# Two-layer pooling and stick-breaking trunk on one core: head sums by an accumulating transfer, and transposes of two blocks together

## The chip, the cores and the metric

The kernel runs on one core of one Trainium2 chip. The metric is device microseconds of one execution. Each core has TensorE (PE in the profile), VectorE (DVE), ScalarE (ACT), GpSimd (POOL) and SyncE (SP), each with a queue of its own that it works off in order, and 16 DMA engines that all queues share.

## The reference, cut to what matters

The input is `x` of 2048 frames by 1024 channels. Layer 0 is a gated pooling mixer; layer 1 is the attention that the change touches. Both end in a residual and a gated embedding ("PLE").

```python
q, z = jnp.split(rms_norm(x, b_norm[j]) @ b_w_in[j], 2, axis=-1)
q = rms_norm(split_heads(q), b_q_norm[j])            # 16 heads of 64
o = stick_breaking_attention(q, k_sh, v_sh)
x = x + (o * jax.nn.silu(z)) @ b_w_out[j]            # output projection
x = x + (p[i] @ ple_w[i]) * jax.nn.sigmoid(x @ ple_gate_w[i])

# stick-breaking, strictly causal, per head:
# A[t,s] = beta[t,s] * prod_{s<j<t} (1 - beta[t,j]),  beta = sigmoid(q.k / 8)
```

## The kernel before, in words

Layer 0 and the projections to q, k and v fill the first half of the span (lines before 855); nothing of them is touched. From about 1345 us the attention runs in four stretches, one for each chunk `c` of 512 queries, in the order 3, 2, 1, 0. A chunk has 16 heads, and each head goes over the key chunks `kc` from `c` down to 0. Such a (chunk, head, key chunk) is a slot: 64, 48, 32 and 16 slots in the four stretches.

A slot is worked in four steps `n`, one for each block of 128 queries. Three lags run side by side in one loop (from line 1197):

- `front` (L917 to L941), at step n: two matmuls (L924, L925) give the logits of a block in `psl`, ACT makes `kap`, the sigmoid of minus the logits (L928), and DVE runs the product along the keys into `pp` (a scan, L936, or L933 for the diagonal slot, whose blocks are 128, 256, 384 and 512 wide).
- `turn` (L943 to L954), six steps later: PE transposes up to four 128x128 pieces of `pp` into one PSUM tile `psa` (L949, pool of two buffers), ACT copies it to `at` (L952), and DVE stores the rest that the copy rounds off (L953).
- `gather` (L956 to L981), eight steps after `front`: two matmuls (L961, L962) with stored differences of v add to `pso`.

After a head's last gather ACT copies the two halves of `pso` to `ob` and `os` (L976, L977; the two products of a head lie in different halves of the partitions). For the second head of a pair DVE adds `ob` to `os` (L979), ACT adds a bias in four pieces (`gated`, L972), POOL multiplies by the gate `zt` that SP loaded (L974), and ACT and POOL later split the result into the pair `og` (L1006, L1007) for the output projection. These are put off by `soon(k, ...)`, which runs its function k steps later.

Beside the attention a generator feeds dense matmuls (L994, L996, L998), a few at each step: the gate projection `gate_z` (DVE L1028, ACT L1032, POOL L1033), and `post(c)`, which does the output projection, the gate and the embedding of the chunk that is just finished (DVE L1068 and L1109, POOL L1076 and, for chunks 3 and 2, POOL's accumulating transfer to the output, L1119). `shares` spreads the dense matmuls over the steps of a stretch by a cost model; `even` is a constant rate for the later stretches. `stops[c]` is the step at which chunk c is expected to be done. When all eight `os` of a chunk are appended, the rest of the filler is emptied and the next one begins. After the loop `post(0)` runs alone.

Instructions are put in order engine by engine by a scheduler that may shift those that are not held by `keep_in_program_order`, so small shifts of unrelated instructions come with any edit.

Of the kernel before, what the change touches and what calls it, by code (L numbers as in the profile page):

```python
# [30 lines left out]
def f(ap):  # L31
    return ap.bitcast(F32)
# [3 lines left out]
def trunk_kernel(ctx, tc, x, xt, pt0, wut, cols, heads, zin, grp, aout, agate, aple,  # L36
# [819 lines left out]
    with ExitStack() as st:  # L856
# [20 lines left out]
        def soon(k, fn):  # L877

            if tail[0]:
                fn()  # L880
                return lambda: None
            item = (now[0] + k, len(due), fn)
            due.append(item)

            def force():
                if item in due:
                    due.remove(item)
                    fn()

            return force  # L890
# [52 lines left out]
        def turn(st, kt):  # L943

            j0 = kt if st["diag"] else 0
            pt = psa.tile([P, W5], F32, tag="psa", name="psa")
            for j in range(j0, 4):
                pp, r0 = st["a"][j]
                T.transpose(pt[:, j * P : (j + 1) * P], pp[:, r0 + kt * P : r0 + (kt + 1) * P], ident)  # L949
            at = t2.tile([P, 2, W5], F32R, tag="at", name="at", bufs=3)  # L950
            cs = slice(j0 * P, W5)
            A.copy(out=at[:, 0, cs], in_=pt[:, cs])  # L952
            V.tensor_tensor(out=at[:, 1, cs], in0=pt[:, cs], in1=f(at[:, 0, cs]), op=ALU.subtract)  # L953
            st["at"][kt] = at  # L954

        def gather(st, kt):  # L956
# [6 lines left out]
            if st["last"] and kt == 3:  # L963
# [12 lines left out]
                soon(1, lambda: stay(A.copy(out=ob[mine], in_=po[other])))  # L976
                soon(2, lambda: stay(A.copy(out=os[mine], in_=po[mine])))  # L977
                if half:
                    soon(3, lambda: V.tensor_tensor(out=os, in0=os, in1=ob, op=ALU.add))  # L979
                    soon(4, gated)  # L980
                    soon(6, lambda: outs[c].append(os))  # L981

        def dense():
            if tail[0] and tail[0] % 4:
# [58 lines left out]

        def post(c):

            pin = t2.tile([P, 2, W5], F32, tag="pin", name="pin", bufs=1)
            nc.sync.dma_start(out=pin, in_=pt0[1, :, c * W5 : (c + 1) * W5].rearrange("(k q) n -> q k n", q=P))
            x3, og, held = [], ogs[c], tc.keep_in_program_order
            while len(og) < 8:
                pair_up(c)  # L1050
            settle()
            both = []
            for o in range(KT):
                xr = t2.tile([P, W5], F32, tag="tmp", name="xr", bufs=4)
                if not c and o < 2:
                    if not o:
# [23 lines left out]
            pt_ = []  # L1080
            for k in range(2):
                pr = t2.tile([P, 2, W5], F32R, tag="ple", name="ple")
                held(A.copy(out=pr[:, 0], in_=pin[:, k]))
                held(V.tensor_tensor(out=pr[:, 1], in0=pin[:, k], in1=f(pr[:, 0]), op=ALU.subtract))
                pt_.append(pr)
            yield
            made()
# [89 lines left out]
        AHEAD = 4  # L1177
        stops = {}
        for n, (c, _, _) in enumerate(slots):
            stops[c] = 4 * (n + 1) + LAG_G + 6  # L1180
        share, even = shares(0, stops[NSUB - 1], NSUB * POSTZ - HELD), 0.0
        done = set()
        ends = {}
# [12 lines left out]

        for n in range(4 * len(slots) + LAG_G):
            now[0] = n
            i2, j2 = divmod(n - LAG_T, 4)
            if 0 <= i2 < len(slots):  # L1200
                turn(active[i2], j2)
            i, j = divmod(n, 4)
            scan = None
            if i < len(slots):
# [37 lines left out]
        for _ in filler:  # L1242
# [54 lines left out]
```

## Time and profile before

| what | value |
|---|---|
| median of three runs | 2690.03 us (2689.37 to 2690.28) |
| the profiled execution's own time | 2688.62 us |
| its span, first to last instruction | 2686.8 us |
| granted TensorE clock, mean over the span | 0.999 |
| PE, DVE, ACT, POOL busy, share of the span | 99%, 72%, 52%, 34% |

The profiled execution's time is 1.8 us above its span. In the page, PE is the row of matmuls and PEld that of the weight loads, which go ahead of their matmuls. The ends of matmuls are modelled, so the distance from one matmul's start to the next says more than its duration. In the view of the waits a row gives the total, the number and the longest of the waits of one line for another.

### The profile page before, as it was taken

How to read it: one execution, taken by the hardware profiler on the slowest of the kernel's cores; microseconds unless marked ns; L12 is line 12 of the kernel's file. 1: busy time of each engine (PE TensorE's matmuls, PEld its weight loads, DVE VectorE, ACT ScalarE, POOL GpSimd, SP SyncE). 2: the span in 40 equal slices, each digit the busy share in tenths (PEclk: the TensorE clock that was granted, in tenths of full speed). 3: DMA queues.
4: the chain of work that ended last, by engine and by line, in shares of the span. 5: the costliest groups of instructions: out<-in, count | busy, mean ns of one | idle time of the engine just before them, and what ended most of it. 6: DMA issues, size and time to landing. Idle time of an engine off the chain costs nothing.

```text
span 2686.8 us, 38640 instructions
## 1 busy us (share of the span) xinstructions
PE 2671.1 (99%) x13352; PEld 2226.1 (83%) x13352; DVE 1926.8 (72%) x2490; ACT 1399.7 (52%) x2735; POOL 909.1 (34%) x724
## 2 busy tenths in 40 slices
PE   9999999999999999999999999999999999999999
PEld 7888888888888888888888888888888888888887
DVE  6776625666357643755499999999999998886632
ACT  6445623455135541445366666666666666665531
POOL 2674338643485434853221111022111111212220
PEclk9999999999999999999999999999999999999999
DMA  8657695567856678443778665555666677768965
GB/s 327 221 176 270 253 308 185 190 237 255 305 176 227 233 249 311 149 151 134 231 231 287 194 208 173 167 169 174 211 183 183 180 211 217 212 204 266 268 222 172
DMA packets 278992, 585.76 MB, mean 218 GB/s; under 512 B 33382, under 2 KB 67430, under 8 KB 278796
## 3 DMA queue, kind: packets, MB, share of 16 engines
q1 hardware_dynamic: 270754, 571.41, 64.6%
q10 hardware_dynamic: 5738, 7.68, 1.1%
q0 software_dynamic: 2304, 4.20, 1.0%
q8 instruction: 106, 1.74, 0.3%
q14 instruction: 90, 0.74, 0.1%
HBM read 438.40 MB, written 136.38 MB: 214 GB/s over the span
## 4 chain that ended last, share of the span: by engine, by line
PE 93%; DVE 4%; DMA 1%; ACT 1%; issue 0%; POOL 0%; SPq 0%; ACTq 0%; DVEq 0%
PE psd L614 19%; PE psd L166 9%; PE psd L167 9%; PE psd L168 9%; PE psa L949 8%; PE psd L994 6%; PE psd L998 6%; PE psd L996 6%; PE psl L925 4%; PE pso L962 4%; PE pso L961 4%; PE psl L924 4%; DVE pp L936 2%; DVE at L953 1%; PE pst L719 1%; PE psdt L994 1%
## 5 line engine op out<-in xcount | busy, mean ns | idle before, releaser
L952 ACT CAST at<-psa 128x512 fp32r<-128x512 f32 (+3 forms) x640 | 334.8, 523 | 430.3 <-PE psa L949 420.7
L614 PE MATMUL psd<-wpair,x 128*128 128x512 f32 x2304 | 536.8, 391 | 0.0
L936 DVE TENSOR_TENSOR_SCAN pp<-kap,pp,zeros 128x512 f32<-128x512 f32 x384 | 512.9, 1336 | 7.5 <-ACT kap L928 6.3
L614 PEld LDWEIGHTS psd<-wpair,x 128*128 128x128 f32 x2304 | 429.9, 188 | 87.0
L953 DVE TENSOR_TENSOR at<-psa,at 128x512 fp32r<-128x512 f32 (+3 forms) x640 | 382.5, 598 | 92.5 <-ACT at L952 87.5
L928 ACT ACTIVATE kap<-psl 128x512 f32<-128x512 f32 (+3 forms) x640 | 344.9, 539 | 13.0 <-PE psl L925 10.1
L949 PE MATMUL psa<-ident,pp 128*128 128x128 f32 x2176 | 344.1, 273 | 4.4 <-DVE at L953 3.8
L949 PEld LDWEIGHTS psa<-ident,pp 128*128 128x128 f32 x2176 | 266.0, 140 | 69.2 <-DVE at L953 12.4
L924 PE MATMUL psl<-kk,qa 128*128 128x512 f32 (+3 forms) x640 | 282.3, 441 | 0.0
L962 PE MATMUL pso<-at,vv 128*128 128x512 f32 (+3 forms) x640 | 234.6, 367 | 1.3 <-DVE at L953 1.3
L925 PE MATMUL psl<-kk,qb 128*128 128x512 f32 (+3 forms) x640 | 232.9, 364 | 0.0
L961 PE MATMUL pso<-at,vv 128*128 128x512 f32 (+3 forms) x640 | 232.7, 364 | 0.1
L933 DVE TENSOR_TENSOR_SCAN pp<-kap,ahead 128x128 f32<-128x128 f32 (+3 forms) x256 | 225.2, 880 | 5.2 <-ACT kap L928 3.2
L167 PE MATMUL psd<-xp,wpair 128*128 128x512 f32 x512 | 199.5, 390 | 1.9 <-DVE xp L316 1.9
L166 PE MATMUL psd<-xp,wpair 128*128 128x512 f32 x512 | 199.8, 391 | 0.8 <-ACT xp L315 0.8
L168 PE MATMUL psd<-xp,wpair 128*128 128x512 f32 x512 | 199.3, 390 | 0.0
L149 DVE SCALAR_TENSOR_TENSOR wpair<-wraw,gains,wpair 128x512 fp32r<-128x512 f32 x192 | 162.5, 888 | 46.6 <-ACT wpair L148 46.1
L143 POOL TENSOR_TENSOR wpair<-wraw,wpair 128x512 fp32r<-128x512 f32 x99 | 144.9, 1473 | 82.0 <-ACT wpair L141 77.4
L148 ACT ACTIVATE wpair<-wraw,gains 128x512 fp32r<-128x512 f32 x192 | 132.9, 719 | 70.2 <-DMA wraw<-in_bq_dram 31.7
L1033 POOL TENSOR_TENSOR zr<-zr,sgz 128x512 f32<-128x512 f32 x32 | 62.0, 1938 | 307.0 <-ACT sgz L1032 273.8
L141 ACT CAST wpair<-wraw 128x512 fp32r<-128x512 f32 x148 | 89.8, 619 | 120.1 <-PE psd L168 89.5
L962 PEld LDWEIGHTS pso<-at,vv 128*128 128x128 f32 x640 | 120.3, 188 | 27.6 <-DVE at L953 1.7
(201 smaller groups left out, 5333.1 us busy)
## 6 DMA issues: line engine op xcount, KB each, us to landing
kk<-kd SPq DMA_DIRECT2D x320, 128.0 KB
vv<-vd SPq DMA_DIRECT2D x160, 256.0 KB
wraw<-in_kv_dram SPq DMA_DIRECT2D x128, 256.0 KB
wpair<-wzd SPq DMA_DIRECT2D x64, 512.0 KB
wpair<-wod SPq DMA_DIRECT2D x64, 512.0 KB
wpair<-wgd SPq DMA_DIRECT2D x64, 512.0 KB
wpair<-wu SPq DMA_DIRECT2D x48, 512.0 KB
wpair<-wi SPq DMA_DIRECT2D x36, 512.0 KB
```

The lines of the kernel that those rows point to most:

```text
L166: T.matmul(ps, wst(units, kt, 0, c0), acts[kt][:, 0], start=(begin and kt == order[0]), stop=False)
L167: T.matmul(ps, wst(units, kt, 0, c0), acts[kt][:, 1], start=False, stop=False)
L168: T.matmul(ps, wst(units, kt, 1, c0), acts[kt][:, 0], start=False, stop=(end and kt == order[-1]))
L614: T.matmul(pss2[i], ck["x2"][kt][:, xh, tk], wst(ws, kt, wh, 0, W5), start=(kt == 0 and xh == 0 and wh == 0), stop=(kt == KT - 1 and wh == 1))
L924: T.matmul(ps[:, :w], qa[:, qs], kk[:, :w], start=True, stop=False)
L925: T.matmul(ps[:, :w], qb[:, qs], kk[:, :w], start=False, stop=True)
L928: A.activation(out=kp[:, r0:], in_=ps[:, :w], func=AF.Sigmoid, scale=-1.0)
L936: V.tensor_tensor_scan(out=pp[:, ::-1], data0=kp[:, ::-1], data1=zeros.to_broadcast([P, W5]), initial=st["carry"][j], op0=ALU.mult, op1=AL ...
L949: T.transpose(pt[:, j * P : (j + 1) * P], pp[:, r0 + kt * P : r0 + (kt + 1) * P], ident)
L953: V.tensor_tensor(out=at[:, 1, cs], in0=pt[:, cs], in1=f(at[:, 0, cs]), op=ALU.subtract)
L961: T.matmul(po[:, cs], vv[:, kt, :], at[:, 0, cs], start=(st["diag"] and kt == 0), stop=False)
L962: T.matmul(po[:, cs], vv[:, kt, :], at[:, 1, cs], start=False, stop=(st["last"] and kt == 3))
```

## The change

Four edits stand in the diff.

1. For chunks 3 and 2 the DVE addition L979 is replaced by a transfer on POOL's queue that adds `ob` to `os` in SBUF (new L980). `gated` then comes 6 steps after the head's end in place of 4, and the appending of `os` 8 in place of 6. Chunks 1 and 0 keep the addition (new L982). `stops` and the constant rate for chunk 1 follow the two steps.
2. From step `by_two` = 464 on, which is the end of chunk 2's last pair, `turn` is called for two blocks at each even step and for none at odd ones. A block with an odd number is thereby transposed one step earlier than before; the gathers stay where they were.
3. `at` gets four buffers in place of three.
4. The embedding input `pin` has no tile of its own any more: it takes two buffers of the four-buffer ring `tmp`, and is loaded by two transfers before the seventh of eight output projections, in place of one transfer at the start of `post`.

```diff
-            at = t2.tile([P, 2, W5], F32R, tag="at", name="at", bufs=3)
+            at = t2.tile([P, 2, W5], F32R, tag="at", name="at", bufs=4)
...
-                    soon(3, lambda: V.tensor_tensor(out=os, in0=os, in1=ob, op=ALU.add))
-                    soon(4, gated)
-                    soon(6, lambda: outs[c].append(os))
+                    if c > 1:
+                        soon(3, lambda: nc.gpsimd.dma_start(out=os, in_=ob, accum_op=ALU.add))
+                    else:
+                        soon(3, lambda: V.tensor_tensor(out=os, in0=os, in1=ob, op=ALU.add))
+                    soon(6 if c > 1 else 4, gated)
+                    soon(8 if c > 1 else 6, lambda: outs[c].append(os))
...
-            pin = t2.tile([P, 2, W5], F32, tag="pin", name="pin", bufs=1)
-            nc.sync.dma_start(out=pin, in_=pt0[1, :, c * W5 : (c + 1) * W5].rearrange("(k q) n -> q k n", q=P))
...
+                if o == KT - 2:
+                    pin = [t2.tile([P, W5], F32, tag="tmp", name="pin", bufs=4) for _ in range(2)]
+                    for k in range(2):
+                        nc.sync.dma_start(out=pin[k], in_=pt0[1, k * P : (k + 1) * P, c * W5 : (c + 1) * W5])
...
-            stops[c] = 4 * (n + 1) + LAG_G + 6
+            stops[c] = 4 * (n + 1) + LAG_G + (8 if c > 1 else 6)
+        by_two = stops[2] // 2 * 2
...
-            i2, j2 = divmod(n - LAG_T, 4)
-            if 0 <= i2 < len(slots):
-                turn(active[i2], j2)
+            for m in (n,) if n < by_two else (n, n + 1) if n % 2 == 0 else ():
+                i2, j2 = divmod(m - LAG_T, 4)
+                if 0 <= i2 < len(slots):
+                    turn(active[i2], j2)
...
-                        even = POST / (64.0 * c - (LAG_G + 2 if c == 1 else 1))
+                        even = POST / (64.0 * c - (LAG_G + 2 if c == 1 else 3))
```

Lines from 979 on carry numbers 3 to 6 higher in the changed kernel; L1035 and L1036 there are L1032 and L1033 here, L1010 is L1007, L997, L999 and L1001 are L994, L996 and L998, L1114, L1118 and L1119 are L1109, L1113 and L1114.

Three places show how instructions move. The first is the end of the second head pair of chunk 3. On ACT before, the bias L972 stands two `kap` behind the copy L977:

```order
L977 COPY os<-pso 64x512
L952 CAST at<-psa 128x512
L928 ACTIVATE kap_12444<-psl 128x512
L952 CAST at<-psa 128x512
L928 ACTIVATE kap_12445<-psl 128x512
L972 ACTIVATE os<-os,en 128x128 x4
```

On ACT in the changed kernel at the same place:

```order
L977 COPY os<-pso 64x512
L952 CAST at<-psa 128x512
L928 ACTIVATE kap_12444<-psl 128x512
L952 CAST at<-psa 128x512
L928 ACTIVATE kap_12445<-psl 128x512
L952 CAST at<-psa 128x512
L928 ACTIVATE kap_12442<-psl 128x512
L1035 ACTIVATE sgz<-zr 128x512
L952 CAST at<-psa 128x512
L928 ACTIVATE kap_12443<-psl 128x512
L972 ACTIVATE os<-os,en 128x128 x4
```

The bias stands four `kap` behind the copy now, two steps later.

On POOL, further on in chunk 3 (`og` is the pair for the output projection, `zr` and `sgz` belong to the gate projection), before:

```order
L1007 TENSOR_TENSOR og<-os,og 128x512
L1033 TENSOR_TENSOR zr<-zr,sgz 128x512
L974 TENSOR_TENSOR os<-os,zt 128x512
L1007 TENSOR_TENSOR og<-os,og 128x512
L1033 TENSOR_TENSOR zr<-zr,sgz 128x512
```

and in the changed kernel:

```order
L1010 TENSOR_TENSOR og<-os,og 128x512
L980 DMA os<-ob 128x512
L1036 TENSOR_TENSOR zr<-zr,sgz 128x512
L974 TENSOR_TENSOR os<-os,zt 128x512
L1010 TENSOR_TENSOR og<-os,og 128x512
L1036 TENSOR_TENSOR zr<-zr,sgz 128x512
```

The new transfer stands ahead of a multiplication that does not belong to it. Of the 16 new transfers, seven are followed by such an instruction and nine by their own L974.

The second place is PE in chunk 1, before:

```order
L949 MATMUL psa<-ident,pp 128x128 x4
L924 MATMUL psl<-kk,qa 128x512
L925 MATMUL psl<-kk,qb 128x512
L994 MATMUL psd<-og,wpair 128x512
L996 MATMUL psd<-og,wpair 128x512
L998 MATMUL psd<-og,wpair 128x512
L961 MATMUL pso<-at,vv 128x512
L962 MATMUL pso<-at,vv 128x512
L949 MATMUL psa<-ident,pp 128x128 x4
```

and in the changed kernel:

```order
L949 MATMUL psa<-ident,pp 128x128 x8
L924 MATMUL psl<-kk,qa 128x512
L925 MATMUL psl<-kk,qb 128x512
L1001 MATMUL psd<-og,wpair 128x512
L997 MATMUL psd<-og,wpair 128x512
L999 MATMUL psd<-og,wpair 128x512
L961 MATMUL pso<-at,vv 128x512
L962 MATMUL pso<-at,vv 128x512
L924 MATMUL psl<-kk,qa 128x512
L925 MATMUL psl<-kk,qb 128x512
```

Two groups of four transposes stand in one run of eight, and the next step begins with its logits.

The third place is DVE at the end of the attention, where the last `at` of chunk 0 are made beside the end of `post(1)` (`sg`, `x`: its gate and its sum), before:

```order
L953 TENSOR_TENSOR at<-psa,at 128x384
L1109 TENSOR_TENSOR sg<-psd,sg 128x512
L953 TENSOR_TENSOR at<-psa,at 128x256
L1114 TENSOR_TENSOR sg<-sg,x_26312 128x512
L953 TENSOR_TENSOR at<-psa,at 128x128
```

and in the changed kernel:

```order
L953 TENSOR_TENSOR at<-psa,at 128x384
L1114 TENSOR_TENSOR sg<-psd,sg 128x512
L953 TENSOR_TENSOR at<-psa,at 128x256
L953 TENSOR_TENSOR at<-psa,at 128x128
L1119 TENSOR_TENSOR sg<-sg,x_26318 128x512
```

The last `at` stands ahead of the sum that waits for POOL, no longer behind it.

More of the change, by code (lines that the diff above doesn't have):

```diff
@@ L1082, in post @@
                 pr = t2.tile([P, 2, W5], F32R, tag="ple", name="ple")
-                held(A.copy(out=pr[:, 0], in_=pin[:, k]))
-                held(V.tensor_tensor(out=pr[:, 1], in0=pin[:, k], in1=f(pr[:, 0]), op=ALU.subtract))
+                held(A.copy(out=pr[:, 0], in_=pin[k]))
+                held(V.tensor_tensor(out=pr[:, 1], in0=pin[k], in1=f(pr[:, 0]), op=ALU.subtract))
                 pt_.append(pr)
```

## Prediction

> **What bounds the kernel now.** I read the page first, for the engines and the chain that ended last.
>
> ```profile
> span 2686.8 us, 38640 instructions
> PE 93%; DVE 4%; DMA 1%; ACT 1%; issue 0%; POOL 0%; SPq 0%; ACTq 0%; DVEq 0%
> ```
>
> PE carries 93% of the chain. The number of matmuls does not change, so the change can only win what PE loses by waiting. Where that is, the view by windows tells, asked for the stretches of chunks 3, 2 and 1 (columns: window, length, then PE, PEld, DVE, ACT and POOL busy with their counts, clock, DMA share, GB/s).
>
> ```profile
> 1345.00:1870.00 525.00, 521.74 (x2881) 434.71 (x2880) 510.77 (x610) 340.70 (x680) 88.88 (x48) 1.00 0.64 201
> 1870.00:2210.00 340.00, 338.53 (x1882) 283.81 (x1881) 326.58 (x399) 225.00 (x466) 55.67 (x37) 1.00 0.64 192
> 2210.00:2435.00 225.00, 224.73 (x1250) 190.47 (x1249) 196.32 (x259) 146.75 (x324) 41.32 (x31) 1.00 0.75 216
> ```
>
> In chunks 3 and 2 (the first two rows) DVE is busy for 97% and 96% of the time, in chunk 1 for 87%, and PE never stands still for long. So DVE and PE run nearly level in chunks 3 and 2, and PE alone bounds chunk 1. Next the waits of PEld for DVE, asked for steps 1405 to 1870 us, 1870 to 2210 us, for 1870 to 1880 us and 2120 to 2210 us alone, and for the end from 2435 us; no such row answers for 2210 to 2435 us.
>
> ```profile
> PEld psa L949 <- DVE at L953: 5.0, 11, 1.6
> ```
> ```profile
> PEld psa L949 <- DVE at L953: 4.9, 9, 0.9
> ```
> ```profile
> PEld psa L949 <- DVE at L953: 1.6, 2, 0.9
> ```
> ```profile
> PEld psa L949 <- DVE at L953: 2.7, 5, 0.7
> ```
> ```profile
> PEld pso L962 <- DVE at L953: 1.7, 1, 1.7
> ```
>
> A wait in this view is longer than what PE loses, since loads run ahead. The longest one, in the timeline, gives the correction:
>
> ```profile
> 1780.43 0.39 PE L962 MATMUL pso<-at,vv 128*128 128x512 f32 x1
> 1781.28 0.67 DVE L953 TENSOR_TENSOR at<-psa,at 128x512 fp32r<-128x512 f32 x1
> 1782.00 0.42 PEld L949 LDWEIGHTS psa<-ident,pp 128*128 128x128 f32 x4 [1.61 <-DVE at L953]
> ```
>
> The transposes start 1.57 us after L962, where a matmul of this width takes 0.23 us from start to start (2354.33 to 2354.56 below). PE lost 1.34 us, the view says 1.61: 0.27 us too much for each wait. So PE lost 5.0 - 11 x 0.27 = 2.0 us in chunk 3 after 1405 us, 4.9 - 9 x 0.27 = 2.5 us in chunk 2, and 1.4 us at the end. That is about 6 us, and almost all that edits 1 and 2 can win.
>
> **The addition taken from DVE.** The addition and the steps around one of them, in chunk 3:
>
> ```profile
> L979 DVE TENSOR_TENSOR os<-os,ob x32: 659/669/1711, 1414.1 to 2585.1; 128x512 f32<-128x512 f32 x32
> 1588.61 0.58 ACT L977 COPY os<-pso 64x512 f32<-64x512 f32 x1
> 1589.96 0.60 ACT L928 ACTIVATE kap<-psl 128x512 f32<-128x512 f32 x1
> 1591.56 1.27 DVE L936 TENSOR_TENSOR_SCAN pp<-kap,pp,zeros 128x512 f32<-128x512 f32 x1
> 1591.79 0.60 ACT L928 ACTIVATE kap<-psl 128x512 f32<-128x512 f32 x1
> 1592.28 0.40 ACT L972 ACTIVATE os<-os,en 128x128 f32<-128x128 f32 x1
> 1871.50 1.71 POOL L1033 TENSOR_TENSOR zr<-zr,sgz 128x512 f32<-128x512 f32 x1 [0.45 <-ACT sgz L1032]
> 1872.05 1.71 DVE L979 TENSOR_TENSOR os<-os,ob 128x512 f32<-128x512 f32 x1
> ```
>
> DVE is rid of 16 x 0.67 us and of the 1.04 us by which the one at 1872 us was stretched beside POOL: 11.7 us. PE gets only what it waits for, and no single removal is worth more to it than its own length. Chunk 3 has eight additions in 525 us, and the two kinds need not meet: of its 2.0 us I count three quarters, 1.5 us, since the 1.34 us at 1780 us are worth one addition's 0.67 us at the most; of the 1.6 us from 1870 to 1880 us, right behind the stretched addition, all 1.1 us that PE lost. Of the five waits from 2120 us on (2.7 - 5 x 0.27 = 1.35 us) I count half, 0.7 us, since scans that POOL stretched (below) stand among their causes. Sum: 3.3 us gained, between nothing and 4.5 us.
>
> By the Trainium skill, SBUF — State Buffer, section "Who interferes with whom", a DVE instruction with two SBUF inputs and a GpSimd instruction that reads SBUF hold each other up, and the first to start has its way. The 1.71 us of L979 beside L1033 agrees with it.
>
> **The accumulating transfer in its place.** ACT must not reach L972 before it lands, since `kap` and the copies to `at` are queued behind L972, and DVE and PE behind those. The only accumulating transfers of before go to HBM:
>
> ```profile
> L1119 POOL DMA_DIRECT2D out_dram<-sg x16: 859/878/1095, 2040.1 to 2430.9; - x16
> DMA to landing us min/median/max: 4.4/5.5/7.7
> ```
>
> L977 ends at 1589.19. L972 comes two `kap` later than before; two of them are 1.83 us apart, so it is due at 1592.28 + 2 x 1.83 = 1595.94, which is 6.75 us after the copy. A landing takes 4.4 to 7.7 us, median 5.5, so the slot holds it in most cases. The latest would be 0.95 us late, and that is still covered: the `kap` that begins at 1589.96 ends at 1590.56, and its scan starts at 1591.56, so DVE runs 1.0 us behind ACT. I take a cost of 0. If POOL is held by an L1033 of 1.71 us ahead of the issue and the landing is the slowest, it is 9.4 us against 7.75: 1.7 us lost. Nothing excludes a landing that is quicker than these rows; it would bring nothing.
>
> The Trainium skill's page DMA: Bandwidth & Descriptors, section "Anatomy of one DMA — SWDGE (gpsimd) path", gives 2.0 us and bytes over 436 GB/s, an estimate of 2.6 us for these 256 KB; the measured 5.5 us is twice that, and the sum goes by the measured one.
>
> The issue itself costs DVE something in some cases. Two issues of L1119, each followed at once by L1007:
>
> ```profile
> 2100.97 0.87 POOL L1119 DMA_DIRECT2D out_dram<-sg  x1 [3.96 <-ACT kap L928]
> 2101.19 1.22 DVE L933 TENSOR_TENSOR_SCAN pp<-kap,ahead 128x512 f32<-128x512 f32 x1
> 2101.61 1.88 POOL L1007 TENSOR_TENSOR og<-os,og 128x512 fp32r<-128x512 f32 x1
> 2121.47 0.88 POOL L1119 DMA_DIRECT2D out_dram<-sg  x1 [17.98 <-PE psa L949]
> 2121.69 2.81 DVE L933 TENSOR_TENSOR_SCAN pp<-kap,ahead 128x384 f32<-128x384 f32 x1
> 2122.08 1.59 POOL L1007 TENSOR_TENSOR og<-os,og 128x512 fp32r<-128x512 f32 x1
> ```
>
> The first scan, 512 wide, took 1.22 us and the second, only 384 wide, 2.81 us: at least 1.6 us more. So an issue with a POOL instruction right behind it can hold a scan. Of the new issues seven have a foreign POOL instruction behind them; by ACT's order only in some four of these its input is ready at once. In chunk 2 the five waits from 2120 us on cost PE 1.35 us, 0.27 us apiece. Four such cost 1.1 us, none costs 0, all seven twice as much each 3.8 us; I take 0.7 us.
>
> **Two blocks transposed together.** What a group costs is read from PE's starts, one group of one and one of four:
>
> ```profile
> 2346.24 0.27 PE L949 MATMUL psa<-ident,pp 128*128 128x128 f32 x1
> 2346.27 0.36 PE L924 MATMUL psl<-kk,qa 128*128 128x256 f32 x1
> 2346.47 0.28 PE L925 MATMUL psl<-kk,qb 128*128 128x256 f32 x1
> 2346.59 0.40 PE L998 MATMUL psd<-x,wpair 128*128 128x512 f32 x1
> 2353.66 0.60 PE L949 MATMUL psa<-ident,pp 128*128 128x128 f32 x4
> 2354.01 0.48 PE L924 MATMUL psl<-kk,qa 128*128 128x512 f32 x1
> 2354.33 0.39 PE L925 MATMUL psl<-kk,qb 128*128 128x512 f32 x1
> 2354.56 0.39 PE L996 MATMUL psd<-x,wpair 128*128 128x512 f32 x1
> ```
>
> One transpose: 0.03 us to L924, and L924 takes 0.20 us where L925 of the same width takes 0.12, together 0.11 us. Four: 0.35 us, and L924 takes 0.32 us against 0.23, together 0.44 us, again 0.11 apiece. A group has no price of its own, so the 91 pairs save PE nothing. They might cost: both `psa` buffers must be free at once. Two steps lie between a buffer's uses, 3.5 us (chunk 1's 225 us hold 128 steps), and the second block's stores end about one copy (0.52 us) and one L953 (0.67 us) later than before; chunk 1 has 13% of DVE's time free, which hides it. I take 0; with that cover gone, 0.1 us in each of 91 pairs would be 9 us. An advantage is excluded by the rows, but for the end:
>
> ```profile
> L952 ACT CAST at<-psa 128x512 fp32r<-128x512 f32 (+3 forms) x640 | 334.8, 523 | 430.3 <-PE psa L949 420.7
> 2582.60 0.69 DVE L1114 TENSOR_TENSOR sg<-sg,x 128x512 f32<-128x512 f32 x1 [1.90 <-POOL sg L1113]
> 2583.21 0.28 DVE L953 TENSOR_TENSOR at<-psa,at 128x128 fp32r<-128x128 f32 x1
> ```
>
> The last L953 stands behind L1114, which waits 1.90 us for POOL. In the changed order it stands ahead of it, and the 1.4 us go. Late next is the chain of the last two blocks itself, two copies and two L953 of 0.3 to 0.4 us that gathers of 0.8 us cover in part: 0.2 us. Gain 1.2 us, between 0.5 and 1.7.
>
> **Buffers and loads.** The fourth `at` buffer only holds what the earlier transposes make. The `pin` loads move on SP behind the weights of the sixth projection. Their two `tmp` buffers last held `xr` of projections three and four, done two projections before, and their data are used three projections later; the ring leaves `xr` one projection of prefetch. Both 0, with a PE wait for `xr` as the price of failure; a stretch with DVE at 97% would show it.
>
> **Sum.** 3.3 + 1.2 - 0.7 = 3.8 us. The profiled execution, 2688.6 us (1.8 us above its span), would come to 2684.8, and the median, 1.4 us higher, from 2690.0 to **2686.2 us**.
>
> **Rivals.**
>
> *All of it goes.* If DVE's 11.7 us open so much room that no wait is left in chunks 3 and 2 and at the end, 2.0 + 2.5 + 1.4 = 5.9 us, with the waits ahead of 1405 us one or two more: about 2683.5. For it: DVE and PE run within 3 to 4% of each other. Against: waits behind stretched scans remain.
>
> *The work comes back on DVE.* If POOL's issues hold scans (1.6 us x 7 = 11.2 us against 11.7 us saved), chunks 3 and 2 stay as they are and only the end is won: 2690.0 - 1.2, about 2689. The two rows of L1119 speak for both.
>
> *The transfer lands late*, which ends slower. ACT stands at L972, `kap` behind it, DVE runs dry after its 1.0 us, then PE. The turning point is a mean landing of 7.75 us after the copy. At 9 us it costs 16 x 1.25 = 20 us, less 4.5 gained: about 2705. The median landing of 5.5 us speaks against it; that POOL can be 1.7 us late, and that DMA engines are 64% busy, for it. The Trainium skill's SBUF — State Buffer, section "SBUF: two separate sides", warns that a DVE instruction of a two-port mode keeps GpSimd from writing descriptors (0.62 us becoming 3.1 us). The issues of L1119 took 0.86 to 1.10 us in stretches with DVE 87 to 96% busy, so the trace does not bear it out for this DVE work.
>
> *The change does nothing measurable besides*, because scheduling shifts give back what it wins: 2690, with the forecast in the same class.
>
> **How the numbers follow.** The forecast has 0.45, the full gain 0.2, the two cases near 2689 to 2690 together 0.22, the late landing 0.13. What a measurement of this kernel can tell from no change is about 0.2%, 5.4 us. Faster by that needs under 2684.7: the full gain and the lower edge of the forecast, 0.22 in all. Slower needs over 2695.4: the late landing, 0.11 of its 0.13. Same has 0.67. The range goes from 2681.5 (all gains and the waits ahead of 1405 us) to 2692 (the work back on DVE and a lost microsecond or two); the late landing beyond it and edges are the 2 in 10 left out.
>
> **What would show it.** Right: no L979 in DVE's rows before 2200 us, DVE's busy time there 10 us down; PEld's waits for L953 falling from 9.9 to about 4 us between 1405 and 2210 us; ACT idle ahead of L972 near nothing; eight transposes in about 0.83 us to the next L924; no wait at the last L962. Wrong: an ACT wait for the transfer at L972; scans of 2 us and more beside the new issues; PE waits for `psa` between 2210 and 2435 us.

## The result and the profile after

The changed kernel took 2683.89 us (median of 12 runs, 2681.82 to 2685.63) and the kernel before 2689.26 us beside it (12 runs, 2688.38 to 2690.28): a ratio of 0.9979, 95% interval 0.9971 to 0.9986, or 5.4 us. In a second comparison (11 runs against 21) it was 2683.19 against 2688.93 us, 0.9976 (0.9967 to 0.9985). The forecast was 3.8 us less, with 2681.5 to 2692.0 as its range.

The page of the profiled execution answers to that of before with its span and its chain:

```profile
span 2682.4 us, 39425 instructions
PE 96%; DMA 1%; DVE 1%; issue 0%; ACT 0%; SPq 0%; ACTq 0%; DVEq 0%
```

DVE has fallen from 4% of the chain to 1%, and PE carries what DVE gave up. The windows, with the columns of before:

```profile
1345.00:1870.00 525.00, 521.11 (x2884) 435.09 (x2882) 507.98 (x603) 340.92 (x681) 91.60 (x56) 1.00 0.67 204
1870.00:2210.00 340.00, 339.89 (x1899) 286.83 (x1898) 317.64 (x394) 227.71 (x473) 61.44 (x45) 1.00 0.70 200
2210.00:2435.00 225.00, 224.66 (x1248) 192.45 (x1247) 195.44 (x258) 143.17 (x320) 41.63 (x31) 1.00 0.75 215
```

DVE is busy 2.8 us less in the first row and 8.9 us less in the second. PE's share rises in the second row alone, where its work of 340 us now leaves 0.1 us free in place of 1.5. The waits of PEld for DVE say the same, first for 1405 to 1870 us, then for 1870 to 2210 us:

```profile
PEld psa L949 <- DVE at L953: 4.0, 6, 1.0
```
```profile
PEld psa L949 <- DVE at L953: 0.8, 2, 0.4
```

Less 0.27 us for each wait, chunk 3 has 4.0 - 6 x 0.27 = 2.4 us where it had 2.0, and chunk 2 has 0.8 - 2 x 0.27 = 0.3 us where it had 2.5. Uncorrected that is 4.8 us, where the prediction named about 4. So the gain of the attention lies in chunk 2, and chunk 3 gave none. From 2210 to 2435 us, where no row of this kind stood before, there is one now:

```profile
PEld psa L949 <- DVE at L953: 0.7, 1, 0.7
```

The prediction named such a wait as a sign of being wrong. Edit 1 alone has it too (0.6 us in two waits), so the pairs do not make it.

The transfers (L980) and the bias behind them (L972), each asked by its line:

```profile
L980 POOL DMA_DIRECT2D os<-ob x16: 862/878/1092, 1414.1 to 2176.1; - x16
DMA to landing us min/median/max: 3.3/4.2/8.3
```
```profile
  DMA os<-ob: 1.4, 1
```

Fifteen of the 16 landed before ACT came to L972; one kept ACT waiting, 1.4 us, which is the other sign of that kind. At the end of the attention, DVE and PE in the timeline:

```profile
2577.27 0.69 DVE L1114 TENSOR_TENSOR sg<-psd,sg 128x512 f32<-128x512 f32 x1 [2.20 <-ACT sg L1100]
2578.04 0.62 DVE L953 TENSOR_TENSOR at<-psa,at 128x256 fp32r<-128x256 f32 x2
...
2578.74 0.22 PE L961 MATMUL pso<-at,vv 128*128 128x128 f32 x1
2578.80 0.27 PE L962 MATMUL pso<-at,vv 128*128 128x128 f32 x1
...
2580.23 0.69 DVE L1119 TENSOR_TENSOR sg<-sg,x 128x512 f32<-128x512 f32 x1 [1.57 <-POOL sg L1118]
```

Both of the last L953 (x2) end before the sum that waits for POOL, and the last L962 follows its L961 by 0.06 us, where before it had waited 1.28 us.

To place the difference, I compare two marks on PE: the first logits of the attention and the last matmul of the kernel, before and after (both kernels have 13352 matmuls).

```profile
1332.78 0.22 PE L924 MATMUL psl<-kk,qa 128*128 128x128 f32 x1
...
2681.50 0.39 PE L998 MATMUL psd<-ple,wpair 128*128 128x512 f32 x1
```
```profile
1333.08 0.22 PE L924 MATMUL psl<-kk,qa 128*128 128x128 f32 x1
...
2677.37 0.39 PE L1001 MATMUL psd<-ple,wpair 128*128 128x512 f32 x1
```

That distance went from 1348.7 to 1344.3 us, 4.4 us less. It leaves out what differs in the profiled executions ahead of the attention and in the last output. In the table below it is split at the start of step 255 (the end of chunk 3) and of step 512 (in chunk 1, past chunk 2's post-processing). Where a kernel appends two steps later, dense matmuls have moved behind these marks; their number, four at step 255 and five at step 512, was counted in the trace and 0.23 us added for each. Where pairs are made there, one more transpose stands ahead of step 512, and 0.11 us is taken off for it.

### The profile page after: what moved, and what is told of

It reads as the page before. It is cut to its first block, busy times and chain, and to the rows that moved or that the text cites. A ratio compares the mean times of both kernels' runs of the same rounds, so it can differ in the third digit from the quotient of the medians.

```text
span 2682.4 us, 39425 instructions
## 1 busy us (share of the span) xinstructions
PE 2669.6 (100%) x13352; PEld 2230.8 (83%) x13352; DVE 1907.9 (71%) x2474; ACT 1397.0 (52%) x2735; POOL 919.7 (34%) x740
## 4 chain that ended last, share of the span: by engine, by line
PE 96%; DMA 1%; DVE 1%; issue 0%; ACT 0%; SPq 0%; ACTq 0%; DVEq 0%
PE psd L614 19%; PE psd L167 9%; PE psd L166 9%; PE psd L168 9%; PE psa L949 9%; PE psd L997 6%; PE psd L1001 6%; PE psd L999 6%; PE psl L925 5%; PE pso L962 5%; PE psl L924 5%; PE pso L961 5%; PE pst L719 1%; PE psdt L997 1%; PE psdt L1001 1%; PE psdt L999 1%
## 5 line engine op out<-in xcount | busy, mean ns | idle before, releaser
L952 ACT CAST at<-psa 128x512 fp32r<-128x512 f32 (+3 forms) x640 | 325.5, 523 | 350.1 <-PE psa L949 340.0
L953 DVE TENSOR_TENSOR at<-psa,at 128x512 fp32r<-128x512 f32 (+3 forms) x640 | 375.0, 598 | 70.0 <-ACT at L952 64.7
L949 PE MATMUL psa<-ident,pp 128*128 128x128 f32 x2176 | 329.3, 273 | 3.4 <-DVE at L953 3.0
L924 PE MATMUL psl<-kk,qa 128*128 128x512 f32 (+3 forms) x640 | 274.9, 430 | 0.3 <-DMA kk<-kd 0.3
L962 PE MATMUL pso<-at,vv 128*128 128x512 f32 (+3 forms) x640 | 234.0, 366 | 0.0
L961 PE MATMUL pso<-at,vv 128*128 128x512 f32 (+3 forms) x640 | 232.3, 363 | 0.0
L143 POOL TENSOR_TENSOR wpair<-wraw,wpair 128x512 fp32r<-128x512 f32 x99 | 145.2, 1475 | 82.0 <-ACT wpair L141 81.4
L1036 POOL TENSOR_TENSOR zr<-zr,sgz 128x512 f32<-128x512 f32 x32 | 59.6, 1861 | 266.4 <-ACT sgz L1035 246.8
L962 PEld LDWEIGHTS pso<-at,vv 128*128 128x128 f32 x640 | 120.3, 188 | 26.1
```

Source lines behind the costliest of these rows:

```text
L924: T.matmul(ps[:, :w], qa[:, qs], kk[:, :w], start=True, stop=False)
L961: T.matmul(po[:, cs], vv[:, kt, :], at[:, 0, cs], start=(st["diag"] and kt == 0), stop=False)
L962: T.matmul(po[:, cs], vv[:, kt, :], at[:, 1, cs], start=False, stop=(st["last"] and kt == 3))
```

## The experiments

All medians are of 11 runs in five rounds (of 12 in the changed kernel's first row, of 5 in the row of transfers with old steps), with the kernel before run between them on the same chip. An interval of 0.09% on either side is 2.4 us, so the medians alone do not tell differences of two microseconds apart, and PE's marks are shown beside them. The last three columns are differences from the kernel before along PE's marks, from one profile each, in us: chunk 3, chunk 2 to step 512, and from there to the last matmul. The changed kernel's second profile shows how far two profiles of one kernel differ: by up to half a microsecond in a column.

| kernel | median, us | before beside it | ratio (95%) | chunk 3 | chunk 2 | rest |
|---|---|---|---|---|---|---|
| changed kernel | 2683.89 | 2689.26 | 0.9979 (0.9971 to 0.9986) | +0.2 | -2.8 | -1.8 |
| changed kernel again | 2683.19 | 2688.93 | 0.9976 (0.9967 to 0.9985) | -0.3 | -2.8 | -2.1 |
| edit 1 alone | 2686.52 | 2689.17 | 0.9988 (0.9979 to 0.9997) | -0.1 | -2.8 | -0.4 |
| edits 2 to 4 alone | 2687.05 | 2689.17 | 0.9991 (0.9982 to 1.0000) | 0.0 | -0.7 | -1.6 |
| edits 3 and 4 alone | 2689.10 | 2689.17 | 1.0000 (0.9991 to 1.0009) | +0.3 | 0.0 | +0.2 |
| addition left out | 2687.29 | 2689.17 | 0.9993 (0.9984 to 1.0002) | -1.4 | -1.6 | +0.1 |
| later steps, DVE adds | 2689.80 | 2689.16 | 1.0003 (0.9994 to 1.0012) | +2.0 | -1.1 | +1.2 |
| pairs at the last slot alone | 2686.83 | 2689.16 | 0.9991 (0.9983 to 1.0000) | -0.3 | -0.1 | -1.5 |
| pairs from the start | 2686.03 | 2689.20 | 0.9986 (0.9977 to 0.9995) | +1.1 | -0.5 | -2.1 |
| transfers in all chunks | 2694.81 | 2689.20 | 1.0021 (1.0012 to 1.0029) | -0.6 | -2.9 | +9.8 |
| transfers, old steps | 2705.97 | 2689.16 | 1.0062 (1.0048 to 1.0075) | +13.9 | +2.3 | 0.0 |
| first pair added on DVE | 2683.54 | 2689.16 | 0.9978 (0.9970 to 0.9987) | -0.6 | -2.8 | -2.1 |
| the same, pairs at the last slot | 2683.75 | 2688.93 | 0.9979 (0.9970 to 0.9988) | +0.2 | -2.7 | -2.2 |

### The edits apart

Edit 1 alone, on the kernel before:

```diff
-                    soon(3, lambda: V.tensor_tensor(out=os, in0=os, in1=ob, op=ALU.add))
-                    soon(4, gated)
-                    soon(6, lambda: outs[c].append(os))
+                    if c > 1:
+                        soon(3, lambda: nc.gpsimd.dma_start(out=os, in_=ob, accum_op=ALU.add))
...
+                    soon(6 if c > 1 else 4, gated)
+                    soon(8 if c > 1 else 6, lambda: outs[c].append(os))
...
-                        even = POST / (64.0 * c - (LAG_G + 2 if c == 1 else 1))
+                        even = POST / (64.0 * c - (LAG_G + 2 if c == 1 else 3))
```

> Edit 1 alone: accumulating transfers for chunks 3 and 2 with their two later steps; single transposes and the old buffers. Relief theory (DVE freed of 11.7 us in chunks 3 and 2 lets PE wait less there, the pairs win only at the end of the attention): 2.6 us below before, PE waits for L953 in chunk 2 falling from 4.9 to about 1 us as in the changed kernel, and the 1.4 us at the last L962 still there. Pair theory (the gain is made by the pairs in chunks 1 and 0): within 1 us of before. Shuffle theory (any edit shifts neighbours, and the gain is that of one lucky order): anything from 4 us below to 2 us above, not repeated by the runs without the addition.

It gained 2.65 us. As expected, PEld's waits for L953 in chunk 2 fell to the 0.8 us of the changed kernel, and the wait of 1.7 us at the last L962 stayed. Edits 2 to 4 alone, with the DVE addition kept:

```diff
+        by_two = stops[2] // 2 * 2
...
+            for m in (n,) if n < by_two else (n, n + 1) if n % 2 == 0 else ():
+                i2, j2 = divmod(m - LAG_T, 4)
```

> Edits 2 to 4 alone: pairs of transposes from step 462 on, four buffers, the moved embedding load; the DVE addition stays. Relief theory: 1.2 to 1.6 us below before, all of it at the last gathers, with chunks 3 and 2 as before (PE waits for L953 of about 5 us in each). Pair theory: 4 to 5 us below before. Shuffle theory: no forecast.

They gained 2.1 us, more than the 1.2 to 1.6 us expected and less than the 4 to 5 us of the pair theory; PEld's waits for L953 stay at 5.0 us in chunk 3 and fall only to 4.1 us in chunk 2. Together the parts give 4.8 of the 5.4 us; nothing shows that the two edits need or hinder each other. The buffers and the loads by themselves (edits 3 and 4, with transposes one block at a time):

```diff
-            at = t2.tile([P, 2, W5], F32R, tag="at", name="at", bufs=3)
+            at = t2.tile([P, 2, W5], F32R, tag="at", name="at", bufs=4)
...
+                if o == KT - 2:
+                    pin = [t2.tile([P, W5], F32, tag="tmp", name="pin", bufs=4) for _ in range(2)]
```

> Edits 3 and 4 alone: four at buffers and the moved embedding load; single transposes and the DVE addition. Relief theory and pair theory: equal to before within 1 us. Shuffle theory: a shift of 2 us or more either way would show that moved transfers alone move the time.

They change nothing: 0.1 us, with an interval of 0.09% on either side. So a shift of transfers and buffers by itself does not make the gain.

### What of edit 1 wins

The addition left out for chunks 3 and 2, with nothing in its place and the old steps; half of each head pair's sum is missing there.

```diff
-                    soon(3, lambda: V.tensor_tensor(out=os, in0=os, in1=ob, op=ALU.add))
+                    if c < 2:
+                        soon(3, lambda: V.tensor_tensor(out=os, in0=os, in1=ob, op=ALU.add))
```

> Before with the addition of the two halves left out for chunks 3 and 2 (half of each pair's sum is missing there, and no transfer takes its place); all steps as before. It bounds what DVE's relief is worth without the transfer's cost. Relief theory: 3 to 4.5 us below before, and no slower than edit 1 alone by more than 1 us, PE waits for L953 in chunks 3 and 2 together under 5 us where before has 9.9. Pair theory: within 1 us of before. Shuffle theory: no common direction with edit 1 alone.

By medians it gained 1.9 us (2.0 without one run of 12597.5 us), less than expected, and its interval reaches 1.0002. PEld's waits for L953 fell to 2.3 us in chunk 3 and 3.1 us in chunk 2, together a little above the 5 us that was expected at most. Along PE's marks it gained 1.4 us in chunk 3 and 1.6 in chunk 2, 3.0 in all; in this profile the last output landed later and took 0.9 us of it back. So DVE's 11.7 us are worth 2 to 3 us to PE, and three of the four stretched scans stay, for instance (timeline, POOL and DVE):

```profile
2118.94 0.88 POOL L1120 DMA_DIRECT2D out_dram<-sg  x1 [17.99 <-PE psa L949]
2119.15 2.81 DVE L933 TENSOR_TENSOR_SCAN pp<-kap,ahead 128x384 f32<-128x384 f32 x1
2119.55 1.59 POOL L1008 TENSOR_TENSOR og<-os,og 128x512 fp32r<-128x512 f32 x1
```

The other half of edit 1, its two later steps, with the addition kept on DVE:

```diff
-                    soon(4, gated)
-                    soon(6, lambda: outs[c].append(os))
+                    soon(6 if c > 1 else 4, gated)
+                    soon(8 if c > 1 else 6, lambda: outs[c].append(os))
```

> The addition stays on DVE, but bias and appending come two steps later, as with the transfers; single transposes, old buffers. It has edit 1's shift of steps and order without its relief of DVE. Relief theory: within 1 us of before, PE waits for L953 in chunk 2 still at 4 us or more. Shuffle theory (the gain of edit 1 comes from the shifted order, such as POOL's transfers to the output and its og split meeting DVE's scans less often): 2 to 3 us below before, and stretched scans beside the output transfers down from 4.

It gained nothing by medians. Against it, edit 1 alone is 2686.52 to 2689.80, 3.3 us lower: with the same steps, that is what taking the addition from DVE brings. By PE's marks the two differ by 3.7 us over chunks 3 and 2; the 1.6 us by which they differ in the last column are no part of it, for there this profile has a wait of 1.3 us of PE for a load of keys, at 2439 us, that edit 1 alone does not have. By PE's marks the later steps lose 2.0 us in chunk 3 and win 1.1 us in chunk 2. The waits of PEld in chunk 3 bear out the loss:

```profile
PEld psa L949 <- DVE at L953: 5.7, 11, 0.8
PEld psa L949 <- ACT rb L1025: 1.6, 3, 0.9
```

The first row had 5.0 us before, and of the second kind (`rb`, a copy of the gate projection on ACT) there was one wait of 0.8 us. Which instruction of the later order makes them, no run here tells apart. This profile was 1.1 us above the kernel's median, so 2.0 us may be an upper reading, although the wait at 2439 us is long enough to account for it. PEld's waits for L953 in chunk 2 were 3.3 us, where 4 or more were expected.

In chunk 2 the later steps change POOL's order, and that shows what became of the stretched scans. Before there were four of them beside output transfers, at 2121, 2143, 2164 and 2188 us, each 1.6 to 1.9 us longer than usual. In the changed kernel, POOL and DVE at the first and the third place, with the issue of a new transfer between them:

```profile
2123.01 1.28 DVE L936 TENSOR_TENSOR_SCAN pp<-kap,pp,zeros 128x512 f32<-128x512 f32 x1
2123.45 1.92 POOL L1010 TENSOR_TENSOR og<-os,og 128x512 fp32r<-128x512 f32 x1 [17.41 <-ACT og L1009]
2125.31 0.89 POOL L1124 DMA_DIRECT2D out_dram<-sg  x1
2125.38 1.28 DVE L936 TENSOR_TENSOR_SCAN pp<-kap,pp,zeros 128x512 f32<-128x512 f32 x1
...
2132.05 1.28 DVE L936 TENSOR_TENSOR_SCAN pp<-kap,pp,zeros 128x512 f32<-128x512 f32 x1
2132.93 0.87 POOL L980 DMA_DIRECT2D os<-ob  x1 [6.72 <-ACT os L977]
2134.14 1.28 DVE L936 TENSOR_TENSOR_SCAN pp<-kap,pp,zeros 128x512 f32<-128x512 f32 x1
...
2166.49 0.86 POOL L1124 DMA_DIRECT2D out_dram<-sg  x1 [18.53 <-DVE sg L1114]
2166.70 1.27 DVE L936 TENSOR_TENSOR_SCAN pp<-kap,pp,zeros 128x512 f32<-128x512 f32 x1
2167.05 2.00 POOL L1010 TENSOR_TENSOR og<-os,og 128x512 fp32r<-128x512 f32 x1
2168.48 1.67 DVE L936 TENSOR_TENSOR_SCAN pp<-kap,pp,zeros 128x512 f32<-128x512 f32 x1
```

At 2123 us L1010 comes ahead of the issue, and both scans take their usual 1.28 us. At 2133 us the new issue leaves the scans at 1.28 us. At 2166 us the issue comes first as before, yet the scan behind it is not held; POOL's L1010 is (2.00 us in place of 1.59), and the next scan by 0.4 us. The kernel with later steps and the DVE addition kept has none of the four stretches either, and the kernel below with the transfers at the old steps has all four, at 2136, 2158, 2179 and 2205 us. So the two later steps removed them, not the transfers.

### How much lateness the transfer may have

Edit 1's transfer with the bias and the appending left at their old steps (`stops` and the rate too):

```diff
-                    soon(3, lambda: V.tensor_tensor(out=os, in0=os, in1=ob, op=ALU.add))
+                    if c > 1:
+                        soon(3, lambda: nc.gpsimd.dma_start(out=os, in_=ob, accum_op=ALU.add))
```

> Edit 1 alone, but bias and appending at their old steps (4 and 6), two steps earlier than with edit 1: L972 is due some 3.1 us after the copy L977 ends, and the transfers land 3.3 to 8.3 us after their issue, median 4.2. Theory of the late landing: ACT waits at nearly every L972, about 1.3 us each; beyond the 1.0 us that DVE runs behind ACT, 0.3 to 0.5 us each reach PE, 16 of them 5 to 8 us, so 3 to 6 us above edit 1 alone, 0 to 4 us above before. Rival, that ACT has room enough (64% busy) to make such waits good: level with edit 1 alone within 1 us.

It took 16.8 us more than the kernel before and 19.5 us more than edit 1 alone, three to six times what was expected. The line of the bias, the landings, and ACT's waits in chunk 3 and in chunk 2:

```profile
  DMA os<-ob: 24.4, 15
...
DMA to landing us min/median/max: 3.3/3.7/8.6
```
```profile
ACT os L972 <- DMA os<-ob: 19.2, 7, 5.9
```
```profile
ACT os L972 <- DMA os<-ob: 5.2, 8, 1.8
```

In chunk 3 seven waits of 2.7 us on average cost PE 13.9 us; less 1.0 us of cover for each, 19.2 - 7 x 1.0 = 12.2 us were to be expected from the waits. But the 13.9 us are not standing alone. Behind the longest wait PE also ran slowly (timeline of PE, then a window):

```profile
1425.55 0.98 PE L949 MATMUL psa<-ident,pp 128*128 128x128 f32 x4 [4.04 <-DVE at L953]
```
```profile
1425.50:1429.20 3.70, 3.65 (x11) 2.98 (x12) 3.70 (x5) 2.00 (x5) 0.15 (x1) 0.54 0.44 172
```

The granted clock was 0.54 there, and the matmuls up to the next transposes took 3.7 us, where the same matmuls from 1419.29 us on took 2.1. Behind the next long wait, 2.75 us at 1606 us, the clock was 0.50 from 1610.7 to 1613.3 us, and some 1.3 us went in the same way. That is 2.9 us by the clock and 11.0 us of standing, or a cover of 1.2 us for each wait. In chunk 2 eight waits of 0.65 us on average, the longest 1.8, mostly stay within that cover, and PE lost 2.3 us. So the late landing is the right mechanism, and the cover of 1.0 us is nearly right; I had taken too short a wait, and nothing for the clock. It also shows that the two later steps are needed: they cost up to 2 us in chunk 3 and save nearly ten times that.

In the changed kernel the one late transfer is the first, issued at 1414 us, where the 16 DMA engines are 91% busy (1390 to 1440 us). The timeline around its end:

```profile
1414.05 1.09 POOL L980 DMA_DIRECT2D os<-ob  x1 [3.45 <-DMA zd<-zr]
...
1422.44 1.28 ACT L972 ACTIVATE os<-os,en 128x128 f32<-128x128 f32 x4 [1.43 <-DMA os<-ob]
...
1424.22 0.69 DVE L953 TENSOR_TENSOR at<-psa,at 128x512 fp32r<-128x512 f32 x1 [1.21 <-ACT at L952]
```

Issue to landing took 8.3 us. POOL was idle for 3.45 us ahead of the issue, but the issue followed the end of the copy L977 (1413.73 us) by 0.3 us, so POOL did not make it late. ACT waited 1.43 us at L972, and DVE stood still 1.21 us (DVE, not PE as the expectation below has it). If that costs PE about 1 us, leaving this one pair to DVE should win it back:

```diff
-                    if c > 1:
+                    if c > 1 and (c, h2) != (NSUB - 1, 0):
...
+                    late = 2 * (c > 1 and (c, h2) != (NSUB - 1, 0))
+                    soon(4 + late, gated)
+                    soon(6 + late, lambda: outs[c].append(os))
```

> The changed kernel, but the first head pair of chunk 3 keeps the DVE addition with its old steps; the other 15 transfers stay. In the changed kernel that first transfer took 8.3 us to land, ACT waited 1.4 us for it at L972, and PE stood 1.2 us a little later. Theory that this one late landing is paid by PE: 1 us below the changed kernel (about 6.4 us below before), no ACT wait for a transfer, chunk 3's early steps level with before. Rival that DVE's relief and not the lateness decides: level with the changed kernel within 0.5 us, as the relief of one addition is lost.

It was 2683.54 us, 0.35 us below the changed kernel, in a comparison of its own. So it was tried again beside the changed kernel, and with pairs of blocks at the last slot alone (`by_two = 642`):

> The changed kernel once more, beside the next one on the same chip, so that the two are compared directly. Both theories: 2683.9 us, as in the first comparison, 5.4 us below the kernel before.

> The changed kernel with two parts put back: the first head pair of chunk 3 keeps the DVE addition and its old steps, and blocks are transposed in pairs only from step 642 on, the end of chunk 0. Theory (the first transfer, which landed after 8.3 us, cost about 1 us; pairs are worth something at the end alone): 2683 us, 0.5 to 1.5 us below the changed kernel beside it, with no ACT wait for a transfer at L972 and no PE wait at the last L962. Rival (pairs in chunk 1 and the first part of chunk 0 are worth something too, and the one late landing was covered elsewhere): 2684 to 2685.5 us, level with the changed kernel or up to 1.5 us above it.

Beside each other they are 2683.19 us (changed) and 2683.75 us: level, the rival's outcome, and no version here beats the changed kernel. PE's waits for DVE between 1400 and 1475 us bound what there was to win. In the changed kernel they were

```profile
PE psa L949 <- DVE at L953: 0.8, 2, 0.6
```

and 0.6 us in its second profile; in both kernels without the late transfer there were none. So the late landing cost PE 0.8 us at the most, which these medians do not tell from nothing. The last kernel also waits 1.2 us for a load of keys, but at 1403 us, ahead of the first transfer, where the other profiles of these kernels show from nothing to 0.6 us, so the transfer that is left out does not make it.

### What the pairs win

Edits 3 and 4 with pairs from step 642 on, which is the last slot alone:

```diff
+        by_two = 642
```

> Edits 3 and 4, and transposes in pairs only from step 642 on, that is for the four blocks of the last slot. Theory: all that the pairs win is the last L953 coming ahead of the sum that waits for POOL, so this gives what the pairs from step 464 on gave, 1.5 to 2.1 us below before, and the last L962 waits no more. Rival: the pairs save PE time all along (2.1 us over 91 pairs, 23 ns each): then two pairs give less than 0.3 us.

It gained 2.3 us, as much as the pairs with edits 2 to 4 and their 2.1 us. A steadier measure is the distance on PE from the last logits to the last matmul, 503 matmuls in each of these kernels: 114.1 us in the kernel before, with edit 1 alone and with edits 3 and 4 alone, and 112.2 us with edits 2 to 4, with the last slot alone and in the changed kernel. That is 1.9 us, and as far as these runs tell, of the 91 pairs only those of the last slot are worth anything. Pairs in all four chunks, on the changed kernel:

```diff
-        by_two = stops[2] // 2 * 2
+        by_two = 0
```

> The changed kernel with transposes in pairs from step 0, so in chunks 3 and 2 too. A step there takes 1.84 us and DVE is busy for 94 to 97% of it; in a pair the second psa buffer is free only after two copies and two stores, and both must be free at once for the next eight transposes. Theory that the pairs are free only where DVE has room: chunks 3 and 2 get slower, PE waits for L953 there rising from 4.8 us to 10 us or more, 3 to 15 us above the changed kernel. Rival, that a pair costs and saves nothing anywhere but at the end: level with the changed kernel within 1 us.

It took 2.1 us more than the changed kernel by medians and 3.0 us by the marks, the right sign with a smaller size than the 3 to 15 us expected. The waits of PEld for `psa` in chunk 2 went from two to nine, in chunk 3 they stayed near 4 us:

```profile
PEld psa L949 <- DVE at L953: 2.6, 9, 0.9
```

A pair itself costs PE nothing, as eight transposes of the changed kernel show (timeline, PE):

```profile
2349.31 1.06 PE L949 MATMUL psa<-ident,pp 128*128 128x128 f32 x8
2350.12 0.48 PE L924 MATMUL psl<-kk,qa 128*128 128x512 f32 x1
2350.44 0.39 PE L925 MATMUL psl<-kk,qb 128*128 128x512 f32 x1
2350.67 0.39 PE L1001 MATMUL psd<-x,wpair 128*128 128x512 f32 x1
```

It is 0.81 us to L924, and L924 takes 0.32 us against 0.23: 0.90 us, or 0.11 us for each transpose, as in ones and fours.

### Transfers for chunks 1 and 0 as well

```diff
-                    if c > 1:
+                    if c >= 0:
...
-                    soon(6 if c > 1 else 4, gated)
-                    soon(8 if c > 1 else 6, lambda: outs[c].append(os))
+                    soon(6, gated)
+                    soon(8, lambda: outs[c].append(os))
```

> The changed kernel with accumulating transfers and later steps for chunks 1 and 0 too (16 more transfers, 16 more DVE additions gone). PE bounds those chunks with DVE 87% and 56% busy, so relief there is worth nothing: level with the changed kernel within 1 us, and at the end of the attention 3 to 5 us of transfer and two more steps stand ahead of the last og, which post(0) uses 9.7 us after its first matmul: up to 3 us worse if that chain outgrows its cover. Rival, that relief is worth as much there as in chunks 3 and 2: 2 to 3 us better than the changed kernel.

It took 10.9 us more than the changed kernel; a difference of 3 us at the most was expected. Up to step 575 nothing is lost along the marks. The last transfer is then on the path that sets the end (timeline of ACT, DVE and PE, then two windows):

```profile
2591.79 0.39 PE L1001 MATMUL psdt<-og,wpair 128*128 128x512 f32 x1
...
2594.19 1.28 ACT L972 ACTIVATE os<-os,en 128x128 f32<-128x128 f32 x4 [8.51 <-DMA os<-ob]
2595.49 0.69 DVE L974 TENSOR_TENSOR os<-os,zt 128x512 f32<-128x512 f32 x1 [9.08 <-ACT os L972]
2596.22 0.62 ACT L1009 CAST og<-os 128x512 fp32r<-128x512 f32 x1 [0.76 <-DVE os L974]
...
2596.89 0.80 PE L997 MATMUL psdt<-og,wpair 128*128 128x512 f32 x1 [4.72 <-ACT og L1009]
...
2602.05 0.40 PE L999 MATMUL psdt<-og,wpair 128*128 128x512 f32 x1
```
```profile
2597.00:2602.00 5.00, 5.00 (x11) 3.69 (x12) 1.95 (x3) 1.24 (x2) 1.69 (x2) 0.50 0.38 118
2602.00:2610.00 8.00, 8.00 (x36) 6.59 (x35) 0.69 (x1) 0.62 (x1) 2.15 (x2) 1.00 0.84 256
```

PE stands from 2591.79 to 2596.89, 4.9 us more than the usual 0.23. Then 11 matmuls take 5.16 us where they would have taken 2.5, at a granted clock of 0.50: 2.6 us more. That is 7.5 of the 10.9 us. The rest goes between steps 575 and 600, where ACT waited 5.70 us at L972 for another transfer and 16 dense matmuls fewer were done in the same time; that this wait is its cause is argued from the place alone.

## Why the prediction was right, and where its sizes were off

- **The addition taken from DVE (forecast 3.3 us, between nothing and 4.5).** Right in mechanism, and in size as far as it can be told: 3.3 us by medians and 3.7 along PE's marks from edit 1 against the same steps with the DVE addition; 1.9 us by medians and 3.0 along PE's marks where the addition is left out. The split holds too: forecast 1.5 us in chunk 3 and 1.8 in chunk 2, shown 1.4 and 1.6 with the addition left out.
- **Issues that hold scans (forecast a loss of 0.7 us).** This step failed. None of the 16 issues stretched a scan by more than 0.4 us on its own account; the one scan of 2 us beside an issue (2.04 us at 1767 us) has its like before, without an issue (2.06 us at 1766 us). The sequence that the term was taken from, a POOL instruction right behind the issue, hardly arose: such an instruction began 0.6 us after the issue in two of the 16 cases, where some four were counted on, and 1.7 to 9.8 us after it in the others. The four stretches that were there before went, through POOL's new order. What cost something was the later order of the bias and the gate, up to 2.0 us in chunk 3. I had followed only ACT's queue position of L972, and given the two steps no price of their own. Loss and gain in part cancel over both chunks, 0.9 us lost along PE's marks and 0.6 us by medians, but they move the gain: all of it came in chunk 2, none in chunk 3. That this net loss comes near the 0.7 us of the forecast is luck, as it has another cause.
- **Lateness (forecast 0).** Right for 15 of 16 transfers. Landings were 4.2 us in the median where the rows of L1119 had 5.5, and the longest was 8.3 where they had 7.7. The late-landing rival did not come about, but its mechanism is real, as the kernel with the old steps shows. The estimate of 2.6 us worked out from the Trainium skill (DMA: Bandwidth & Descriptors, "Anatomy of one DMA — SWDGE (gpsimd) path") lies below even the quickest of these transfers, 3.3 us, in stretches with the DMA engines 67 and 70% busy.
- **Pairs (forecast 0, the end 1.2 us).** That a pair has no price of its own is shown, and that only the end counts as well. The end was undersized: 1.9 us along PE's marks, 2.1 and 2.3 us by medians, beyond the 1.7 us that bounded it. The wait of 1.4 us that I had read went whole, and I had taken 0.2 us off for what is late next; nothing was. A wait of PEld of 0.3 us for ACT ahead of the last L961, which I had not counted, went too; where the rest comes from stays open.
- **Buffers and loads (forecast 0).** Right, 0.1 us.

Along PE's marks the terms that came are 3.7 us for the addition, 1.9 us for the end and 0.9 us lost by the later steps, together 4.7 us, where the changed kernel's two profiles show 4.4 and 5.1; the parts by medians give 4.8 of 5.4. The forecast had 3.3 + 1.2 - 0.7 = 3.8 us. So the sum came out by its two gains; the loss in it was of the right size for a wrong reason. The rival in which all of it goes, at about 2683.5 us, lies nearer to the measured 2683.89 us than the forecast of 2686.2, but its mechanism did not come: PEld still waits 4.0 us for L953 in chunk 3. The forecast, 0.14% faster, stood within the 0.2% that it called no difference (chance 0.67), and the two comparisons, 0.21% and 0.24%, lie just beyond it.

## What to carry to other kernels

Work taken from a busy engine is worth what the bounding engine waits for it, here 3 of 11.7 us, and a view of the waits with its overstatement taken off sizes that well. A transfer that replaces an instruction needs a slot as long as its slowest landing in the order of every queue that waits for it, here two more steps, and the price of making that slot is to be counted like any other edit. At the end of a program, where no later work covers, the same transfer is the wrong tool (10.9 us lost here), and the order of two instructions can be worth nearly as much as all that is won in the middle, here 1.9 against 2.65 us.

## What the runs showed of the hardware

- After a standstill of PE of 4.7 us the granted TensorE clock was 0.50 for 5.2 us, and matmuls of 512 columns started every 0.43 us in place of 0.23. With the transfers at the old steps it was 0.54 for 3.7 us after 4.0 us of standing, and 0.50 for 2.6 us after 2.75 us of standing, in this case not at once but 1.8 us after PE had begun again, behind a second wait of 0.4 us. The Trainium skill's page TensorE: Matmul & The Clock Gate, "Part 1: The HAM clock gate", gives half the clock after an idle window of about 3.4 us and the full one after as long a busy stretch; the traces agree on the half, but one standstill, of 2.75 us, was shorter than that, and the slow stretches lasted 2.6 to 5.2 us.
- An accumulating transfer of 256 KB within SBUF landed in 3.3 to 8.8 us over all these kernels; in the changed kernel the longest, 8.3 us, was the one issued where the DMA engines were 91% busy.
- A scan behind a POOL issue with a POOL instruction (L1007, which splits `og`) right after it was held by 1.6 to 1.9 us in four places before, and not held at 2101 us of the kernel before nor at 2166 us of the changed kernel, in the same sequence. In these two places the POOL instruction took 1.88 and 2.00 us in place of 1.59. What decides it stays open.
